# Two hybrid decoder layers: each layer's rstd folded into the rotary tables, q and k copied out of PSUM by ScalarE and rotated on VectorE alone

## The chip, the cores and the metric

The kernel runs on one core of a Trainium2 chip. The time is device time in microseconds (us) of one execution, from start to end. Engines are named as in the profile: PE (TensorE), DVE (VectorE), ACT (ScalarE), POOL (GpSimd), SP (SyncE, which here only issues DMAs). They run side by side, each through its own list of instructions in order, and wait for one another by semaphores. L163 is line 163 of the kernel before.

## The reference

x is 512 positions of 2048 channels in float32, and there are two layers. Cut to what is touched:

```
for l in range(2):
    h = rms_norm(x, pre_norm_g[l])
    proj = h @ w_in[l]                      # 2048 x 6656, cut into the ten groups below
    rq, rk, rv, rg, dq, dk, dv, dg, lx, lg  # retention, diff attention, RG-LRU
    ro  = retention(rope(rq), rope(rk), rv)             # 6 heads of 128, chunks of 128
    do  = diff_attention(rope(dq), rope(dk), dv, lam)   # 4 heads, q and k in two halves of 64
    lru = rg_lru(conv4(lx), gates)                      # 768 channels, scan over positions
    mixed = concat(rms_norm(ro) * silu(rg), rms_norm(do) * g * silu(dg), lru * silu(lg))
    x = x + rms_norm(mixed @ w_out[l], post_norm_g[l])

def rope(x):        # cos, sin: per position and channel pair
    x1, x2 = split(x, 2)
    return concat(x1 * cos - x2 * sin, x2 * cos + x1 * sin)
```

rms_norm multiplies each position by a reciprocal root mean square, called rstd below. The kernel multiplies the unscaled x (times the gain) by w_in and applies rstd to the product.

## The kernel before

**Passes.** A layer is 18 passes over weights: dv, dq, dk, lx0, lx4, lx8, rq0, rq4, rq8 (`A_` and `B_` in the list `seq`, by the name of the group and the first of its tiles of 128 channels), rv0, rv4, rv8, dg, and for w_out o0, o1, o2, o3a, o3b. rq0, rq4 and rq8 hold the 12 tiles of rq and rk. A pass is 8 chunks of 24 matmuls (128 x 512 results) that accumulate into up to four PSUM banks named `big`. In form A (dq, dk, lx, rq) the weights are stationary and a bank is 128 channels by 512 positions; in form B it is 128 positions by 512 channels.

**Weights.** Each fp32 product is done as three fp32r ones, from a high part and a remainder of both operands. `load_chunk` brings a chunk (512 KB) by a DMA on SP, ACT casts it to `whi` (L163), and DVE subtracts to get `wlo` (L164). There are three buffers of each; a chunk is loaded two chunks ahead of its use.

**Order.** A scheduler orders DVE, ACT, POOL and PE; chunk loads and evacuations have high priority. SP's order is written by hand. The first chunks go round the banks, the last two (three, for passes with fewer banks) bank by bank, and as a bank is complete its evacuation is issued. The next pass takes the banks in the same order.

**Side work.** All else (rotary work, attention, LRU, retention heads) is written as generators in one queue, `side`. After every second (chunk, bank) step, so after 12 matmuls, `pump` runs the first generator up to its next `yield`; the second starts when the first is done. So the number of yields of a piece sets when everything behind it in the queue starts. `drain` empties the queue ahead of the output passes. The tables and `layer_rstd` are side work too, at a layer's start, and `ready` sets the flag that `wait_ready` looks at.

**What the change touches.** `evac_rope` takes q or k of a tile out of PSUM (`qk`), with rstd along the positions (`rsb`, 128 x 512, the same in each partition), and queues `rope`. That multiplies by the sine with the halves swapped (`rt`, L399 and L400 for retention with halves of 64, L404 for diff attention with quarters of 32; on DVE), multiplies by the cosine (L401, L405; POOL), and adds (L406; POOL for retention, DVE for diff). For diff attention `stack` then makes the fp32r parts: two casts on ACT, and for k two more half tiles, moved by POOL's `tensor_scalar` (L427, L428), and remainders `kl` on DVE (L432, L433).

**What stands around it.** `diff_attention` forms scores `sc` in PSUM (L462, L463), a masked maximum on DVE (L465), the exponential `pr` on ACT (L471), and transposes `wT` (L485), copied by ACT (L487). `evac_lx` and `evac_lg` take the LRU's banks out by a DVE multiply with `rsb`; lg then has a sigmoid on ACT (L642), whose table differs from the exponential's, so that ACT loads a table (`ACT_TABLE_LOAD`) between them. `lru_half` makes the gates (L567 to L616: casts `gwh`, `xh` and sigmoids on ACT, `xc`, `xl` on DVE, matmuls `gate`). The retention heads begin behind rv0's pass, and `evac_rvg` takes rv out by turns on DVE and ACT (L738).

Of the kernel before, what the change touches and what calls it, by code (L numbers as in the profile page):

```python
# [18 lines left out]
ALU = mybir.AluOpType  # L19
# [21 lines left out]
LEAD, SLEAD, RLEAD = 4, 8, 6  # L41
# [54 lines left out]
def tile_hybrid_trunk(ctx, tc, x, xt, pos, ppar, lamqk, w_in, gw, w_out, postg, cp, cm, out):  # L96
# [285 lines left out]
    def lead(n):  # L382
        for _ in range(n):
            yield

    def ready():
        prepared[0] = True
        yield

    def wait_ready():  # L390
        while not prepared[0]:
            yield


    def rope(st, raw, dst, key, kind):
        yield from wait_ready()
        t2 = U("rt2")
        if kind == "ret":
            V.tensor_tensor(t2[64:128, :], raw[0:64, :], sin_r[0:64, :], op=ALU.mult)  # L399
            V.tensor_tensor(t2[0:64, :], raw[64:128, :], sin_r[64:128, :], op=ALU.mult)  # L400
            G.tensor_tensor(raw, raw, cos_r, op=ALU.mult)  # L401
        else:
            for a, b in ((0, 32), (32, 0), (64, 96), (96, 64)):
                V.tensor_tensor(t2[b:b + 32, :], raw[a:a + 32, :], sin_d[a:a + 32, :], op=ALU.mult)  # L404
            G.tensor_tensor(raw, raw, cos_d, op=ALU.mult)  # L405
        (G if kind == 'ret' else V).tensor_tensor(raw, raw, t2, op=ALU.add)  # L406
        if kind == "ret":
            dst[key] = raw
        yield
        if kind != "ret":  # L410
            yield from stack(st, raw, key, kind)
# [3 lines left out]
    def stack(st, nat, h, kind):  # L415
        lo_, hi_ = slice(0, 64), slice(64, 128)
        s0, s1 = U("st", F32R), U("st", F32R)
        if kind == "dq":
            A.copy(s0[lo_, :], nat[lo_, :])
            A.copy(s1[hi_, :], nat[hi_, :])  # L420
            V.tensor_tensor(s0[hi_, :], nat[lo_, :], s0[lo_, :], op=ALU.subtract)
            V.tensor_tensor(s1[lo_, :], nat[hi_, :], s1[hi_, :], op=ALU.subtract)
            st["dqs"][h] = (s0, s1)
        else:
            A.copy(s0[lo_, :], nat[lo_, :])
            A.copy(s1[hi_, :], nat[hi_, :])
            G.tensor_scalar(s0[hi_, :], nat[lo_, :], 1.0, 0.0, op0=ALU.mult, op1=ALU.add)  # L427
            G.tensor_scalar(s1[lo_, :], nat[hi_, :], 1.0, 0.0, op0=ALU.mult, op1=ALU.add)  # L428
            k0, k1 = U("kl", F32R), U("kl", F32R)
            G.memset(k0[hi_, :].bitcast(F32), 0.0)  # L430
            G.memset(k1[lo_, :].bitcast(F32), 0.0)
            V.tensor_tensor(k0[lo_, :], nat[lo_, :], s0[lo_, :], op=ALU.subtract)  # L432
            V.tensor_tensor(k1[hi_, :], nat[hi_, :], s1[hi_, :], op=ALU.subtract)  # L433
            st["dks"][h] = (s0, s1, k0, k1)
        yield

    def evac_rope(st, ps, dst, key, kind):
        raw = U("qk")
        V.tensor_tensor(raw, ps, st["rsb"], op=ALU.mult)
        side.append(rope(st, raw, dst, key, kind))  # L440


# [372 lines left out]

    def new_state():
        return {k: {} for k in ("h", "dq", "dk", "dqs", "dks", "dv", "dg", "lx", "lg", "lh", "rq", "rk", "rv", "rg", "ro",
                                "mix", "y", "ry", "xr", "pg")}

    states = [new_state() for _ in range(DEPTH)]  # L820
    for l in range(DEPTH - 1):
# [77 lines left out]
    def start_norm():  # L899
        nc.sync.dma_start(cmt, cm)  # L900
        acc = {}
        for k in range(NK):
            j = int(k % NPOOL == 1)
            sq = U("xsq")
            A.activation(sq, xts[k], AF.Square)
            if j in acc:
                (V, G)[j].tensor_tensor(acc[j], acc[j], sq, op=ALU.add)
            else:
                acc[j] = sq
            if k % 2:  # L910
                yield
        ps = SM("ssx")
        for tb in range(NT):
            for j in range(2):
                T.matmul(ps[:, tb:tb + 1], lhsT=acc[j][:, tb * P:(tb + 1) * P], rhs=ones,
                         start=(j == 0), stop=(j == 1))
        V.tensor_copy(ssx[:, :, 0], ps[:, :NT])
        V.memset(ssx[:, :, 1:], 0.0)
        yield from layer_rstd(st)
# [15 lines left out]
    for l in range(DEPTH):  # L935
        st = states[l]
        if l == 0:
            side.append(chain(start_norm(), lead(LEAD), tables(), layer_params(0), layer_params(1), ready()))
        else:
            side.append(chain(lead(RLEAD), layer_rstd(st)))  # L940
        for i, (p, tasks) in enumerate(layer_passes[l]):
            if i == 13:
                drain()
            if i in (13, 14, 15, 16):
                n = i - 13
                st["pg"][n] = U("pg")
                nc.sync.dma_start(st["pg"][n], postg[l, n * S:(n + 1) * S].partition_broadcast(P))
            if i == 15:
                side.append(load_x(l, st))
            run_pass(p)  # L950
            for t in tasks:
                side.append(t())
# [97 lines left out]
```

## Time and profile before

| | |
|---|---|
| median of three runs | 1665.0 us (1664.53 to 1665.46) |
| the profiled execution | 1666.37 us, span 1664.4 us, mean granted clock 0.993 |
| busy, share of the span | PE 98%, PEld 81%, DVE 56%, ACT 38%, POOL 16% |
| weights' DMAs | 287 of 512 KB on SP's queue, 3.5 to 3.6 us from issue to landing |
| mean DMA rate | 107 GB/s |

The span runs from the first to the last instruction; 2.0 us of the execution lie around it. PEld is the weight load of PE, which runs beside its matmuls. A row of instruction groups reads: line, engine, operation, out<-in, shapes, count, then busy us and mean ns of one, then idle time of the engine just before them and what ended it.

By the trace layer 0's passes run from 6 to 840 us and layer 1's from 840 to 1655; the rotary work of diff attention lies around 101 to 200 and 931 to 1005, that of retention around 440 to 480 and in the rq and rv passes of layer 1 (1142 to 1323).

### The profile page before, as it was taken

What the parts mean: (1) busy time and instruction counts of PE and PEld (TensorE: products, weight loads), DVE (VectorE), ACT (ScalarE), POOL (GpSimd) and SP (SyncE); (2) the same over time, 40 slices, a digit from 0 to 9 for tenths busy, and PEclk for the clock granted to TensorE, in tenths of its full rate; (3) what the DMA queues carried; (4) which work ended last, traced back from release to release, by engine and by line L of the source; (5) the groups of instructions that cost most, each with busy time, mean ns of one, the idle gap of its engine ahead of it and who ended that gap; (6) DMA issues with size and microseconds to landing.
All of it is one profiled execution on the core that took longest, in us unless ns stands there. A gap on an engine that the chain in (4) does not pass through costs nothing. (4 is left out here: it accounts for less than half of the span.)

```text
span 1664.4 us, 19440 instructions
## 1 busy us (share of the span) xinstructions
PE 1634.2 (98%) x7541; PEld 1349.5 (81%) x7541; DVE 928.7 (56%) x1474; ACT 626.0 (38%) x966; POOL 259.1 (16%) x216
## 2 busy tenths in 40 slices
PE   9999899999999999999999998999999999999997
PEld 7788788787877888888888887888888888888886
DVE  6767765665674444322772776664677544442336
ACT  6232345457212323222662224346541222332233
POOL 0011400111261110000110131003035301100003
PEclk9999999999999999999999999999999999999999
DMA  7233222232322222344643222222323322223635
GB/s 258 79 92 101 89 64 84 89 96 76 102 76 77 76 89 83 107 146 158 222 159 100 89 89 77 76 84 83 92 86 102 101 73 77 91 96 108 196 124 199
DMA packets 54747, 177.50 MB, mean 107 GB/s; under 512 B 6656, under 2 KB 7680, under 8 KB 54656
## 3 DMA queue, kind: packets, MB, share of 16 engines
q1 hardware_dynamic: 52592, 169.94, 32.2%
q0 software_dynamic: 1920, 6.29, 1.0%
q8 instruction: 59, 0.97, 0.2%
q14 instruction: 32, 0.26, 0.1%
q10 hardware_dynamic: 144, 0.04, 0.0%
HBM read 167.86 MB, written 8.39 MB: 106 GB/s over the span
## 5 line engine op out<-in xcount | busy, mean ns | idle before, releaser
L164 DVE TENSOR_TENSOR wlo<-raw,whi 128x1024 fp32r<-128x1024 f32 (+1 forms) x289 | 370.5, 1286 | 426.7 <-ACT whi L163 412.8
L163 ACT CAST whi<-raw 128x1024 fp32r<-128x1024 f32 (+1 forms) x289 | 302.6, 1049 | 630.2 <-PE big L208 549.1
L208 PE MATMUL big<-hhi,whi 128*128 128x512 f32 x1024 | 402.9, 394 | 1.5 <-DVE lx L635 1.5
L208 PE MATMUL big<-hhi,wlo 128*128 128x512 f32 x1024 | 400.6, 391 | 1.6 <-DVE wlo L164 1.6
L208 PE MATMUL big<-hlo,whi 128*128 128x512 f32 x1024 | 400.0, 391 | 0.0
L208 PE MATMUL big<-whi,hhi 128*128 128x512 f32 x640 | 255.3, 401 | 3.7 <-ACT rv L738 2.6
L208 PE MATMUL big<-wlo,hhi 128*128 128x512 f32 x640 | 252.0, 395 | 2.7 <-DVE wlo L164 2.7
L208 PE MATMUL big<-whi,hlo 128*128 128x512 f32 x640 | 251.6, 393 | 0.0
L208 PEld LDWEIGHTS big<-hhi,wlo 128*128 128x128 f32 x1024 | 192.9, 188 | 42.5 <-DVE wlo L164 2.0
L208 PEld LDWEIGHTS big<-hhi,whi 128*128 128x128 f32 x1024 | 193.0, 188 | 41.7 <-DVE lx L635 2.0
L208 PEld LDWEIGHTS big<-hlo,whi 128*128 128x128 f32 x1024 | 193.0, 189 | 38.8
L208 PE MATMUL big<-wlo,mhi 128*128 128x512 f32 x512 | 199.5, 390 | 0.6 <-DVE wlo L164 0.6
L208 PE MATMUL big<-whi,mlo 128*128 128x512 f32 x512 | 199.8, 390 | 0.0
L208 PE MATMUL big<-whi,mhi 128*128 128x512 f32 x512 | 199.8, 390 | 0.0
L208 PEld LDWEIGHTS big<-wlo,hhi 128*128 128x128 f32 x640 | 121.5, 190 | 29.4 <-DVE wlo L164 3.1
L208 PEld LDWEIGHTS big<-whi,hhi 128*128 128x128 f32 x640 | 121.5, 190 | 28.3 <-ACT rv L738 3.0
L208 PEld LDWEIGHTS big<-whi,hlo 128*128 128x128 f32 x640 | 121.6, 190 | 24.2
L208 PEld LDWEIGHTS big<-wlo,mhi 128*128 128x128 f32 x512 | 96.1, 188 | 21.2 <-DVE wlo L164 1.5
L208 PEld LDWEIGHTS big<-whi,mlo 128*128 128x128 f32 x512 | 96.2, 188 | 19.7
L208 PEld LDWEIGHTS big<-whi,mhi 128*128 128x128 f32 x512 | 96.1, 188 | 19.6
L773 POOL TENSOR_TENSOR ry<-sy,mhalf 128x1 f32<-128x1 f32 x8 | 4.7, 585 | 406.7 <-DVE sy L771 406.7
L471 ACT ACTIVATE pr<-sc,mx 128x128 f32<-128x128 f32 (+3 forms) x64 | 33.3, 525 | 75.7 <-DVE mx L468 75.6
(212 smaller groups left out, 1530.0 us busy)
## 6 DMA issues: line engine op xcount, KB each, us to landing
raw<-in_w_in SPq DMA_DIRECT2D x207, 512.0 KB, 3.6
raw<-in_w_out SPq DMA_DIRECT2D x80, 512.0 KB, 3.5
xT<-in_xt SPq DMA_DIRECT2D x16, 256.0 KB, 6.6
xr<-in_x SPq DMA_DIRECT2D x16, 256.0 KB, 5.5
xs<-y POOLq DMA_DIRECT2D x16, 256.0 KB, 3.5
xr<-xs SPq DMA_DIRECT2D x16, 256.0 KB, 5.5
pg<-in_postg SPq DMA_DIRECT2D x8, 256.0 KB, 3.9
out<-y POOLq DMA_DIRECT2D x8, 256.0 KB, 4.5
```

The lines of the kernel that those rows point to most:

```text
L163: last_copy[0] = A.copy(hi[:, a:b, :], raw[:, a:b, :])
L164: V.tensor_tensor(lo[:, a:b, :], raw[:, a:b, :], hi[:, a:b, :], op=ALU.subtract)
L208: T.matmul(ps[b], lhsT=lhsT, rhs=rhs, start=(cnt[b] == 0), stop=(cnt[b] == total - 1))
L471: A.activation(p[:, :n], sc[c][:, :n], AF.Exp, bias=mx[:, c:c + 1], scale=0.125, accum_out=sums[:, h:h + 1])
L773: G.tensor_tensor(st["ry"][tb], ms, mhalf[:, :1], op=ALU.pow)
```

## The change

Once a layer's rstd is there, `scale_tables` multiplies the four tables by `rsb` into tiles of the layer (DVE, four instructions). q and k then leave PSUM by a plain copy on ACT, and `rope` uses the scaled tables, all on DVE: for each tile the sine parts, the cosine multiply and the addition. The two half tiles of k that POOL moved are copied by ACT. `rope` waits for the layer's tables (`turned`) instead of for `ready`, and the scaled tables are given back after 8 diff and 12 retention tiles. The rope of diff attention has one yield more, in the middle of its four quarters.

```
+    def scale_tables(st):
+        yield from wait_ready()
+        for name, table in (("cos_d", cos_d), ("sin_d", sin_d), ("cos_r", cos_r), ("sin_r", sin_r)):
+            st[name] = U(name)
+            V.tensor_tensor(st[name], table, st["rsb"], op=ALU.mult)
+            if name[0] == "s":
+                yield
+        st["turned"] = 0
     def rope(st, raw, dst, key, kind):
-        yield from wait_ready()
+        while st["turned"] is None:
+            yield
         t2 = U("rt2")
         if kind == "ret":
-            V.tensor_tensor(t2[64:128, :], raw[0:64, :], sin_r[0:64, :], op=ALU.mult)
-            V.tensor_tensor(t2[0:64, :], raw[64:128, :], sin_r[64:128, :], op=ALU.mult)
-            G.tensor_tensor(raw, raw, cos_r, op=ALU.mult)
+            cos, sin = st["cos_r"], st["sin_r"]
+            swaps, w = ((0, 64), (64, 0)), 64
         else:
-            for a, b in ((0, 32), (32, 0), (64, 96), (96, 64)):
-                V.tensor_tensor(t2[b:b + 32, :], raw[a:a + 32, :], sin_d[a:a + 32, :], op=ALU.mult)
-            G.tensor_tensor(raw, raw, cos_d, op=ALU.mult)
-        (G if kind == 'ret' else V).tensor_tensor(raw, raw, t2, op=ALU.add)
+            cos, sin = st["cos_d"], st["sin_d"]
+            swaps, w = ((0, 32), (32, 0), (64, 96), (96, 64)), 32
+        for a, b in swaps:
+            V.tensor_tensor(t2[b:b + w, :], raw[a:a + w, :], sin[a:a + w, :], op=ALU.mult)
+            if w == 32 and a == 32:
+                yield
+        V.tensor_tensor(raw, raw, cos, op=ALU.mult)
+        V.tensor_tensor(raw, raw, t2, op=ALU.add)
+        st["turned"] += 1
...
     def stack(st, nat, h, kind):
...
-            G.tensor_scalar(s0[hi_, :], nat[lo_, :], 1.0, 0.0, op0=ALU.mult, op1=ALU.add)
-            G.tensor_scalar(s1[lo_, :], nat[hi_, :], 1.0, 0.0, op0=ALU.mult, op1=ALU.add)
+            A.copy(s0[hi_, :], nat[lo_, :])
+            A.copy(s1[lo_, :], nat[hi_, :])
...
     def evac_rope(st, ps, dst, key, kind):
         raw = U("qk")
-        V.tensor_tensor(raw, ps, st["rsb"], op=ALU.mult)
+        A.copy(raw, ps)
         side.append(rope(st, raw, dst, key, kind))
...
-            side.append(chain(start_norm(), lead(LEAD), tables(), layer_params(0), layer_params(1), ready()))
+            side.append(chain(start_norm(), lead(LEAD), tables(), layer_params(0), layer_params(1), ready(), scale_tables(st)))
...
-            side.append(chain(lead(RLEAD), layer_rstd(st)))
+            side.append(chain(lead(RLEAD), layer_rstd(st), scale_tables(st)))
```

PE and SP have the same instructions as before, but the extra yields shift side work against the passes: the first scores of layer 0 move from early in lx4's pass to behind its fifth chunk, the gates from rq0's second chunk to its seventh, the first retention heads from rv4's second chunk to its seventh; in layer 1 the first scores move by two chunks, within lx0's pass. The order in which the instructions stand, at three places (line numbers of the changed kernel are higher; `x2` marks two rows alike):

DVE at layer 0's retention ropes, in rv0's pass, between two weight remainders; before:

```order
L164 TENSOR_TENSOR wlo_3671<-raw_3669,whi_3670 128x1024
L399 TENSOR_TENSOR rt_700_3687<-qk_2984,sin_r 64x512
L400 TENSOR_TENSOR rt_700_3687<-qk_2984,sin_r 64x512
L399 TENSOR_TENSOR rt_704_3722<-qk_3291,sin_r 64x512
L400 TENSOR_TENSOR rt_704_3722<-qk_3291,sin_r 64x512
L399 TENSOR_TENSOR rt_708_3757<-qk_3314,sin_r 64x512
L400 TENSOR_TENSOR rt_708_3757<-qk_3314,sin_r 64x512
L399 TENSOR_TENSOR rt_712_3792<-qk_3334,sin_r 64x512
L164 TENSOR_TENSOR wlo_3706<-raw_3704,whi_3705 128x1024
```

and now:

```order
L164 TENSOR_TENSOR wlo_3689<-raw_3687,whi_3688 128x1024
L420 TENSOR_TENSOR qk_2878<-qk_2878,rt_707_3740 128x512
L416 TENSOR_TENSOR rt_711_3775<-qk_2897,sin_r_1106 64x512
L416 TENSOR_TENSOR rt_715_3810<-qk_2916,sin_r_1106 64x512
L419 TENSOR_TENSOR qk_2897<-qk_2897,cos_r_1104 128x512
L416 TENSOR_TENSOR rt_715_3810<-qk_2916,sin_r_1106 64x512
L420 TENSOR_TENSOR qk_2897<-qk_2897,rt_711_3775 128x512
L419 TENSOR_TENSOR qk_2916<-qk_2916,cos_r_1104 128x512
L164 TENSOR_TENSOR wlo_3724<-raw_3722,whi_3723 128x1024
```

Three and a half ropes' sine halves stood there; now it is less than two whole ropes.

ACT at the end of lx8's pass in layer 0, ahead of rq0's; before:

```order
L163 CAST whi_2525<-raw_2524 128x1024
L642 ACT_TABLE_LOAD
L642 ACTIVATE lgs_2550<-lg_2548 128x512
L642 ACTIVATE lgs_2567<-lg_2565 128x512
L567 CAST gwh_2571<-gwr_2570 96x384
L163 CAST whi_2537<-raw_2536 128x1024
```

and now:

```order
L163 CAST whi_2399<-raw_2398 128x1024
L661 ACT_TABLE_LOAD
L661 ACTIVATE lgs_2424<-lg_2422 128x512
L490 ACT_TABLE_LOAD
L490 ACTIVATE pr_2437,s_443_2357<-sc_2428,mx_2427 128x512
L490 ACTIVATE pr_2439,s_444_2358<-sc_2431,mx_2427 128x512
L506 COPY wT_2450<-wT_2445 128x512
L520 ACTIVATE dsq_2457<-acc_2266 128x512
L661 ACT_TABLE_LOAD
L661 ACTIVATE lgs_2485<-lg_2483 128x512
L661 ACTIVATE lgs_2502<-lg_2500 128x512
L163 CAST whi_2411<-raw_2410 128x1024
```

The attention of layer 0 now runs into this boundary, so that its exponentials alternate with the sigmoids of lg, each with a table load.

DVE at the end of layer 1's diff ropes, in lx0's pass; before:

```order
L406 TENSOR_TENSOR qk_7381<-qk_7381,rt_1310_7515 128x512
L432 TENSOR_TENSOR kl_7546<-qk_7381,st_7540 64x512
L433 TENSOR_TENSOR kl_7547<-qk_7381,st_7541 64x512
L164 TENSOR_TENSOR wlo_7566<-raw_7564,whi_7565 128x1024
L465 ISA sc_7585,mx_7584<-sc_7585,cmt 128x128
```

and now:

```order
L451 TENSOR_TENSOR kl_7622<-qk_7397,st_7616 64x512
L452 TENSOR_TENSOR kl_7623<-qk_7397,st_7617 64x512
L164 TENSOR_TENSOR wlo_7563<-raw_7561,whi_7562 128x1024
L164 TENSOR_TENSOR wlo_7600<-raw_7598,whi_7599 128x1024
L164 TENSOR_TENSOR wlo_7642<-raw_7640,whi_7641 128x1024
L654 TENSOR_TENSOR lx_7664<-big_7399,rsb_6746 128x512
L484 ISA sc_7669,mx_7668<-sc_7669,cmt 128x128
```

Three weight remainders and a bank's evacuation stand between the last rope and the first scores, where there was one remainder.

More of the change, by code (lines that the diff above doesn't have):

```diff
@@ L392, in wait_ready @@
             yield
+    def scale_tables(st):
[6 more added lines that the diff above has]
+        st["turned"] = 0
     def rope(st, raw, dst, key, kind):
-        yield from wait_ready()
+        while st["turned"] is None:
+            yield
         t2 = U("rt2")
         if kind == "ret":
-            V.tensor_tensor(t2[64:128, :], raw[0:64, :], sin_r[0:64, :], op=ALU.mult)
-            V.tensor_tensor(t2[0:64, :], raw[64:128, :], sin_r[64:128, :], op=ALU.mult)
-            G.tensor_tensor(raw, raw, cos_r, op=ALU.mult)
-        else:
-            for a, b in ((0, 32), (32, 0), (64, 96), (96, 64)):
-                V.tensor_tensor(t2[b:b + 32, :], raw[a:a + 32, :], sin_d[a:a + 32, :], op=ALU.mult)
-            G.tensor_tensor(raw, raw, cos_d, op=ALU.mult)
-        (G if kind == 'ret' else V).tensor_tensor(raw, raw, t2, op=ALU.add)
+            cos, sin = st["cos_r"], st["sin_r"]
+            swaps, w = ((0, 64), (64, 0)), 64
+        else:
+            cos, sin = st["cos_d"], st["sin_d"]
[7 more added lines that the diff above has]
+        st["turned"] += 1
+        if st["turned"] == 8:
+            del st["cos_d"], st["sin_d"]
+        elif st["turned"] == 20:
+            del st["cos_r"], st["sin_r"]
         if kind == "ret":
@@ L817, in new_state @@
         return {k: {} for k in ("h", "dq", "dk", "dqs", "dks", "dv", "dg", "lx", "lg", "lh", "rq", "rk", "rv", "rg", "ro",
-                                "mix", "y", "ry", "xr", "pg")}
+                                "mix", "y", "ry", "xr", "pg")} | {"turned": None}
     states = [new_state() for _ in range(DEPTH)]
```

## The prediction

> **What bounds the kernel now.** First the page: span, busy row of the engines, granted clock.
>
> ```profile
> span 1664.4 us, 19440 instructions
> ...
> PE 1634.2 (98%) x7541; PEld 1349.5 (81%) x7541; DVE 928.7 (56%) x1474; ACT 626.0 (38%) x966; POOL 259.1 (16%) x216
> ```
>
> PE is busy 98% of the span and no other engine is near it, so the time is PE's work plus PE's holes. The change leaves PE's instructions alone; it can only open or close holes. The view of waits for PE names them:
>
> ```profile
> PE sc L462 <- ACT pr L471: 5.2, 3, 2.8
> PE big L208 <- DVE wlo L164: 4.9, 4, 2.7
> PE big L208 <- ACT rv L738: 2.6, 1, 2.6
> PE big L208 <- DVE lx L635: 1.5, 1, 1.5
> ```
>
> Columns: total us, times, longest. Next I looked for the places, and asked the windows view for each: length, busy time of each engine (instructions), granted clock, DMA share, GB/s.
>
> ```profile
> 176.00:182.00 6.00, 4.40 (x20) 3.32 (x19) 5.13 (x7) 1.13 (x2) 2.29 (x4) 1.00 0.11 16
> 192.00:200.00 8.00, 4.74 (x25) 3.63 (x24) 6.38 (x11) 4.39 (x7) 5.74 (x5) 1.00 0.43 128
> 200.00:212.00 12.00, 11.44 (x60) 9.02 (x59) 7.50 (x32) 4.77 (x19) 0.00 (x0) 1.00 0.28 87
> 430.00:440.00 10.00, 10.00 (x46) 8.29 (x45) 2.31 (x2) 1.45 (x2) 0.00 (x0) 1.00 0.35 105
> 470.00:481.00 11.00, 8.30 (x30) 6.35 (x29) 9.93 (x5) 1.05 (x1) 8.74 (x5) 0.84 0.30 90
> 500.00:510.00 10.00, 7.41 (x26) 5.65 (x25) 5.65 (x6) 3.77 (x6) 3.59 (x3) 0.84 0.34 105
> 1000.00:1012.00 12.00, 8.52 (x29) 6.71 (x28) 6.87 (x21) 6.27 (x14) 2.66 (x4) 0.72 0.37 124
> ```
>
> 430 to 440 is an undisturbed stage: PE busy 10.00 of 10, clock 1.00. A disturbed one loses its length less PE's busy time, and beside it (1 - clock) x length, because after the long waits the granted clock stays low for a while. 470-481: 2.70 + 1.76 = 4.46. 500-510: 2.59 + 1.60 = 4.19. 1000-1012: 3.48 + 3.36 = 6.84. 176-182: 1.60; 192-200: 3.26; 200-212: 0.56, all three at full clock. Together 20.9 us; this is what the change can win here. In 192-200, 470-481 and 176-182 POOL and DVE are busy together, and there the durations of DVE give the cause. Groups of one stretch, before and during POOL's work (430 to 453, then 453 to 476; busy us, mean ns):
>
> ```profile
> L400 DVE TENSOR_TENSOR rt<-qk,sin_r 64x512 f32<-64x512 f32 x2 | 1.4, 686 | 0.0
> ...
> L400 DVE TENSOR_TENSOR rt<-qk,sin_r 64x512 f32<-64x512 f32 x6 | 9.1, 1516 | 0.1
> L164 DVE TENSOR_TENSOR wlo<-raw,whi 128x1024 fp32r<-128x1024 f32 x4 | 8.3, 2096 | 0.1
> L399 DVE TENSOR_TENSOR rt<-qk,sin_r 64x512 f32<-64x512 f32 x6 | 8.0, 1340 | 0.2
> ```
>
> And single ones in order of time (start, duration, engine):
>
> ```profile
> 443.98 0.69 DVE L400 TENSOR_TENSOR rt<-qk,sin_r 64x512 f32<-64x512 f32 x1
> ...
> 444.75 1.30 POOL L401 TENSOR_TENSOR qk<-qk,cos_r 128x512 f32<-128x512 f32 x1 [15.54 <-DVE rt L400]
> ...
> 456.21 1.73 POOL L401 TENSOR_TENSOR qk<-qk,cos_r 128x512 f32<-128x512 f32 x1 [1.39 <-PE big L208]
> ...
> 456.80 1.69 DVE L400 TENSOR_TENSOR rt<-qk,sin_r 64x512 f32<-64x512 f32 x1
> ```
>
> The same instruction takes 0.69 us while POOL stands idle (15.54 up to 444.75) and 1.69 inside POOL's multiply of 456.21; the weight remainder wlo takes 2096 ns in that stretch (1290 on average, below). Eight of a chunk's 24 matmuls read wlo, so a DVE at half speed makes wlo late: the hole at 470-481.
>
> **The change part by part.** Prices, from the groups (busy, mean ns, then idle before):
>
> ```profile
> L164 DVE TENSOR_TENSOR wlo<-raw,whi 128x1024 fp32r<-128x1024 f32 x287 | 369.1, 1290 | 426.7 <-ACT whi L163 412.8 <-DMA xr<-xs 7.6 <-DMA xr<-in_x 3.4
> L439 DVE TENSOR_TENSOR qk<-big,rsb 128x512 f32<-128x512 f32 x40 | 27.4, 688 | 22.7 <-PE big L208 22.5
> L406 DVE TENSOR_TENSOR qk<-qk,rt 128x512 f32<-128x512 f32 x16 | 11.1, 691 | 17.4 <-POOL qk L405 17.4
> L401 POOL TENSOR_TENSOR qk<-qk,cos_r 128x512 f32<-128x512 f32 x24 | 44.0, 1834 | 95.6 <-DVE rt L400 92.8 <-PE big L208 2.8
> L406 POOL TENSOR_TENSOR qk<-qk,rt 128x512 f32<-128x512 f32 x24 | 42.6, 1776 | 1.9
> L405 POOL TENSOR_TENSOR qk<-qk,cos_d 128x512 f32<-128x512 f32 x16 | 23.6, 1473 | 169.7 <-DVE rt L404 167.4 <-issue 2.3
> L428 POOL TENSOR_SCALAR st<-qk 64x512 fp32r<-64x512 f32 x8 | 9.6, 1202 | 0.6
> L427 POOL TENSOR_SCALAR st<-qk 64x512 fp32r<-64x512 f32 x8 | 8.6, 1070 | 6.7 <-DVE qk L406 5.8 <-issue 0.9
> L425 ACT CAST st<-qk 64x512 fp32r<-64x512 f32 x8 | 5.0, 621 | 42.1 <-DVE qk L406 42.1
> L487 ACT COPY wT<-wT 128x512 f32<-128x512 f32 x8 | 4.7, 585 | 3.1 <-PE wT L485 3.1
> L642 ACT ACT_TABLE_LOAD x5 | 6.4, 1283 | 2.7 <-DVE lg L640 2.6
> ```
>
> *POOL* loses 40 cos multiplies, 24 additions and 16 half copies: 44.0 + 42.6 + 23.6 + 9.6 + 8.6 = 128.4 of its 259.1 us. Its own time buys nothing; what counts is that DVE's neighbours return to their undisturbed durations, and that a rope no longer waits for POOL (17.4 us of DVE idle behind L405).
>
> *DVE* loses 40 PSUM multiplies (27.4) and gains 8 table multiplies (two layers, four tables; 8 x 0.69 = 5.5), 40 cos multiplies (27.6) and 24 additions (16.6): +22.3. Against that, in 453-476 alone twelve halves shrink from 17.1 to 12 x 0.686 = 8.2. So DVE's total stays within some 20 us of its 928.7, 56% of the span. In the retention ropes' stage the changed order has at most eight rope instructions between two wlo of the main phase, 8 x 0.69 = 5.5 plus one undisturbed wlo of at most 1.29, against the chunk in which they are needed:
>
> ```profile
> 455.93 1.06 ACT L163 CAST whi<-raw 128x1024 fp32r<-128x1024 f32 x1 [4.38 <-PE big L208]
> ...
> 461.37 1.06 ACT L163 CAST whi<-raw 128x1024 fp32r<-128x1024 f32 x1 [4.38 <-PE big L208]
> ```
>
> one chunk every 5.44 us. That is an excess of 1.3 in a chunk or two, with three weight buffers ahead; before, seven rope halves at some 1.43 (the mean of the two rows) and a wlo of 2.10 made 12.1. I cost the DVE side of this at nothing; if that cover fails, wlo is late again by the excess, 1 to 3 us.
>
> *The rstd factor* goes into the tables once a layer, in the stage of the first passes, where nothing waits for the 4 x 0.69 us but the ropes themselves; nothing.
>
> *ScalarE* gains 40 PSUM copies (nearest row L487: PSUM source, 128x512, 585 ns; 23.4 us), 16 half casts (L425, 10.0) and 8 table loads (the order has 40 instead of 32; 10.3): +43.7 on 626, 40%. The total hides under PE; the places don't all. The copy frees the PSUM bank that the next pass needs, and stands in ACT's order behind whatever ACT waits for. Its range: a gain where before a DVE multiply (688) was queued behind wlo, a loss of a whole ACT queue where a gate or softmax stands ahead.
>
> *The moved work.* A rope of diff attention yields once more, so the attention of layer 0 starts some five chunks (27 us) later, in lx4's pass instead of at its start, and the gates and retention heads follow, to rq0 and rv4; layer 1's attention by two chunks. The drain ahead of the output projections stays where it is, so no work is pushed behind the last matmul: the end of the kernel costs nothing either way. But the stall places change. What the shift takes away is in the windows 192-200 (attention start beside POOL's ropes), 500-510 (rv evacuation behind retention heads on ACT) and 1000-1012 (attention start of layer 1), where the cause of the wait can be read:
>
> ```profile
> 1002.52 1.28 ACT L471 ACT_TABLE_LOAD   x1
> ...
> 1005.05 0.39 PE L462 MATMUL sc<-st,st 128*128 128x128 f32 x1 [2.80 <-ACT pr L471]
> ```
>
> There the score matmul waits 2.80 for an exponential that starts behind a table load. In the changed order DVE finishes all ropes of layer 1, then three wlo in a row, ahead of the first scores, so PE has chunk work between them.
>
> What comes instead I walked through by the changed order with the durations above. An attention start costs PE one late probability tile or two (an exp with its 1.28 table load, less the 12 matmuls between two side steps): 1.1 in layer 0 and 1.3 in layer 1. At the boundaries of the LRU and rq passes a copy (0.585) stands behind gate work of 0.6 to 0.7 or a table load of 1.28 on ACT: 1.3 (lx8 to rq0, layer 0), 0.35 (rq4 to rq8), 1.2 (rq0 to rq4, layer 1). The rv evacuation keeps 0.4. Sum 5.65. Each of these six is unseen in the trace; bounds by the nearest rows are nothing (430-440) and 4.19 (500-510, a bank released late by ACT, with its clock). I take values near the lower end because the clock fell only behind waits of 2.6 us and more, and the walked waits are half of that; the upper end goes into the range.
>
> A table load's price decides part of that. In the trace the next instruction starts 1.30 after it:
>
> ```profile
> 100.53 1.28 ACT L294 ACT_TABLE_LOAD   x1
> 101.83 0.63 ACT L294 ACTIVATE sin_r<-ang 64x512 f32<-64x512 f32 x1
> ```
>
> The Trainium skill, "ScalarE: Activation LUTs", section "What ACT_TABLE_LOAD costs", adds a drain of about 1380 ns to every switch, 2.66 us in all; by it, as an estimate, the eight new loads would be 21.3 us of ACT instead of 10.3, and the three at lx8 to rq0 would hold that boundary's copies 4.1 longer. The 1.30 of the row leaves no room for that drain, and I go by the row.
>
> Sum: gone 20.9, new 5.65, net 15.2, taken as 15. The profiled execution took 1666.4 for a span of 1664.4, and the sum is made against it: 1651.4. It is 1.4 above the median of the three runs (1665.0); against that median, 1650.0.
>
> **The rivals.**
>
> *PSUM held by ScalarE (slower).* ACT works in order; the forty copies wait behind sigmoids, exponentials, casts and table loads at five boundaries (lx8 to rq0, rq0 to rq4 and rq4 to rq8 in layer 0; lx8 to rq0 and rq0 to rq4 in layer 1), which before were DVE's. If each costs what 500-510 cost, 4.19, the result is 1650 - 2.85 (what the forecast has there) + 21 = 1668; at 6.84 (as 1000-1012) 1681. I put it at 1672. It decides from (15 + 2.85) / 5 = 3.6 us a place. For it: ACT's idle time 42.1 behind DVE at L425 shows that its queue does stand and wait. Against it: the last two chunks go bank by bank, so a pass's first bank is done 36 matmuls, 8.2 us, before the next pass starts, and its last one is wanted 18 matmuls, 4.1 us, after (by the 5.44 us a chunk); a copy has to be later than that.
>
> *The waits only move (no change).* The wait at 1005 comes from the chain score, exponential, transpose, not from a rope. If such chains reopen at their new places with a low clock, the 20.9 return: 1662 to 1668.
>
> *A part stays.* One of the three long holes keeps its wait and its clock (4.2 to 6.8 us), or table loads hold ACT longer than their row: 1650 + 4 to 11, 1654 to 1661, say 1657. For it: ACT's load rises at just these places.
>
> *POOL is not the cause.* If the half multiplies are slow of themselves, all four DVE instructions of a retention rope would take 1.4, 5.7 together, and a rope can come with every half chunk, 2.72 us: twelve ropes put DVE some 36 us behind, against two chunks (10.9) of weights ahead. The 9.3 of the three POOL windows would not come back, and about 25 would be added: 1650 + 9 + 25 = 1684. Against it: 0.69 and 1.69 in one and the same line.
>
> *More than forecast.* The new waits hide entirely and smaller old holes close too: 1642 to 1645.
>
> **How the numbers follow.** Forecast (gain 10 to 20, 1645 to 1655) 0.53; a part stays 0.20; more 0.07; the waits only move 0.08, all of it within 0.2% (3.3 us, what a measurement of this kernel can tell from none); ScalarE holds PSUM 0.10; POOL not the cause 0.02. Faster 0.53 + 0.20 + 0.07 = 0.80, same 0.08, slower 0.12. The range 1642 to 1664 takes in the first three cases and the lower part of the fourth, a little over 0.8. The forecast alone: 1645 to 1655.
>
> **What would show it.** Right: POOL near 130 us, the retention halves (64x512 by sin_r) near 0.69 on average, ACT near 670, no clock slice below full between 460 and 520 nor near 1005, and PE's waits for wlo and rv gone from the list, with the score waits below 2 us. Wrong: PE waiting for ACT's qk copies in the big rows, a hole of over 2.5 us at a pass boundary between lx8 and rq8, a table load with more than 1.3 us behind it, or half multiplies still above 1 us with POOL idle.
>
> The clock is what doubles a mistake. It fell after holes of 2.59 and 2.70 us here and stayed at full after those of 1.60. The Trainium skill, "TensorE: Matmul & The Clock Gate", section "Why this matters for your kernels", warns of gaps over about 3 us; by that rule a new wait under 3 us would cost only itself, while by these rows one of 2.6 costs 1.6 to 1.8 more.

## The result and the profile after

The changed kernel takes 1642.87 us (median of four runs, 1641.95 to 1643.69), the kernel before 1665.23 in the same set. The ratio is 0.9863, 95% interval 0.9851 to 0.9874: 22.4 us faster, where 15 were forecast. The time lies in the stated range of 1642 to 1664, at its lower end. The profiled execution took 1641.95, 0.9 below the median.

The page of the changed kernel, span and busy row:

```profile
span 1640.2 us, 19391 instructions
...
PE 1625.5 (99%) x7541; PEld 1343.5 (82%) x7541; DVE 905.0 (55%) x1506; ACT 668.4 (41%) x1030; POOL 130.5 (8%) x136
```

The span is 24.2 us shorter. PE's busy time fell by 8.7 with the same 7541 matmuls: those are the stretches at half clock that are gone, some 1.8 us of them at the start (below). PE's idle time, span less busy, fell from 30.2 to 14.7. POOL is at 130.5 and ACT at 668.4, as worked out (130.7 and about 670). DVE has 32 instructions more and 23.7 us less.

PE's waits after:

```profile
PE ssx L934 <- DVE xsq L926: 1.4, 1, 1.4
...
PE big L208 <- DVE wlo L164: 0.8, 2, 0.5
PE sc L481 <- ACT pr L490: 0.8, 2, 0.7
```

The score waits of 5.2 are 0.8, wlo's 4.9 are 0.8, the rv wait of 2.6 and the lx wait of 1.5 are no longer in the list (the prediction had wlo gone from it too); and no wait for a copy of q or k has come in. The windows view by stage shows where the time went. Before (start to the end of dv; lx passes, rq passes and rv passes of layer 0; lx passes of layer 1):

```profile
0.00:57.40 57.40, 53.51 (x222) 41.98 (x223) 35.48 (x50) 31.58 (x48) 6.12 (x11) 0.94 0.56 196
...
144.40:307.00 162.60, 156.81 (x762) 129.83 (x761) 107.40 (x237) 68.11 (x133) 32.08 (x30) 1.00 0.26 80
307.00:450.60 143.60, 143.02 (x626) 115.42 (x625) 91.47 (x113) 76.04 (x99) 26.75 (x19) 1.00 0.29 90
450.60:611.90 161.30, 156.01 (x764) 131.02 (x763) 88.00 (x124) 41.40 (x57) 44.45 (x28) 0.98 0.26 79
...
974.30:1142.00 167.70, 163.17 (x780) 135.40 (x779) 109.04 (x240) 71.97 (x141) 25.61 (x26) 0.98 0.25 78
```

The same five after:

```profile
0.00:55.40 55.40, 52.44 (x222) 40.37 (x223) 35.10 (x49) 31.17 (x47) 6.12 (x11) 0.97 0.57 203
...
142.50:294.50 152.00, 151.30 (x726) 125.83 (x725) 106.84 (x227) 72.89 (x133) 11.02 (x11) 1.00 0.27 83
294.50:441.00 146.50, 146.50 (x662) 120.14 (x661) 83.20 (x113) 89.72 (x122) 18.07 (x14) 1.00 0.29 91
441.00:593.20 152.20, 152.20 (x764) 128.83 (x763) 90.72 (x154) 44.09 (x62) 8.62 (x8) 1.00 0.26 83
...
955.20:1113.90 158.70, 157.66 (x769) 130.94 (x768) 107.69 (x239) 73.37 (x141) 7.88 (x7) 1.00 0.26 82
```

A stage's length says little, since the moved side work puts 36 matmuls into rq that stood in lx; length less PE busy is what counts. In the last four stages it was 5.79 + 0.58 + 5.29 + 4.53 = 16.2 and is 0.70 + 0 + 0 + 1.04 = 1.7. The two stages at 0.98 lost 6.6 us to the clock (0.02 x 161.3 + 0.02 x 167.7) and are at 1.00. So 21.1 us come from these four stages. The start adds 2.0 (57.4 to 55.4) by a part that the change does not touch: the low clock at 50 us lasted half as long in this execution, 3.4 us instead of 6.8. Every profile of this case shows one of these two lengths there, worth 1.7 or 3.4 us. What sets it is not shown, so a difference of 1.7 us between two profiles below may be no more than this.

DVE in layer 0's retention stage (441 to 497) of the changed kernel, where POOL now stands idle:

```profile
L416 DVE TENSOR_TENSOR rt<-qk,sin_r 64x512 f32<-64x512 f32 x20 | 13.7, 686 | 0.5
L164 DVE TENSOR_TENSOR wlo<-raw,whi 128x1024 fp32r<-128x1024 f32 x11 | 13.4, 1222 | 12.6 <-ACT whi L163 12.5
```

The halves take 686 ns, where the stretch before had 1340 and 1516, and wlo 1222 where it had 2096.

### The profile page after: what moved, and what is told of

Its sections match the earlier page's. It is cut to its first block, busy times and chain, and to the rows that moved or that the text cites. A ratio compares the mean times of both kernels' runs of the same rounds, so it can differ in the third digit from the quotient of the medians.

```text
span 1640.2 us, 19391 instructions
## 1 busy us (share of the span) xinstructions
PE 1625.5 (99%) x7541; PEld 1343.5 (82%) x7541; DVE 905.0 (55%) x1506; ACT 668.4 (41%) x1030; POOL 130.5 (8%) x136
## 5 line engine op out<-in xcount | busy, mean ns | idle before, releaser
L164 DVE TENSOR_TENSOR wlo<-raw,whi 128x1024 fp32r<-128x1024 f32 (+1 forms) x289 | 355.7, 1234 | 466.6 <-ACT whi L163 450.5
L208 PEld LDWEIGHTS big<-whi,hlo 128*128 128x128 f32 x640 | 120.7, 189 | 23.7
L416 DVE TENSOR_TENSOR rt<-qk,sin_d 32x512 f32<-32x512 f32 x64 | 43.7, 683 | 3.6 <-ACT qk L458 2.5
```

Source lines behind the costliest of these rows:

```text
L164: V.tensor_tensor(lo[:, a:b, :], raw[:, a:b, :], hi[:, a:b, :], op=ALU.subtract)
L208: T.matmul(ps[b], lhsT=lhsT, rhs=rhs, start=(cnt[b] == 0), stop=(cnt[b] == total - 1))
L416: V.tensor_tensor(t2[b:b + w, :], raw[a:a + w, :], sin[a:a + w, :], op=ALU.mult)
```

## The experiments

The change has four parts: the rope on DVE alone, the extra yield, the tables with ScalarE's copies, and k's halves on ScalarE. Seven kernels put them in or leave them out, so that each ratio to the kernel before can be set against another.

**The rope on DVE alone.** The kernel before with

```
-            G.tensor_tensor(raw, raw, cos_r, op=ALU.mult)
+            V.tensor_tensor(raw, raw, cos_r, op=ALU.mult)
...
-            G.tensor_tensor(raw, raw, cos_d, op=ALU.mult)
-        (G if kind == 'ret' else V).tensor_tensor(raw, raw, t2, op=ALU.add)
+            V.tensor_tensor(raw, raw, cos_d, op=ALU.mult)
+        V.tensor_tensor(raw, raw, t2, op=ALU.add)
```

> The kernel before with one edit: the rope's cosine multiply and addition go from POOL to DVE for all tiles; PSUM evacuation by DVE with rstd, k's halves on POOL and the yields stay, so the side work keeps its places. Theory C (POOL's tensor_tensors slow DVE, and that made the holes): the holes at 179, 194 and 472 (with the low clock behind it) go, 1.8 + 1.7 + 4.5, perhaps the one at 502 (4.2) too; those at the attention starts (198: 1.9; 1002: about 6.8 with the clock) stay. 1652 to 1658. Theory S (the extra yields' shift of the side work is the gain): no change beyond 2 us, 1663 to 1667. If DVE becomes too full instead: above 1667.

1650.48 us, 0.9914 (0.9900 to 0.9927): 14.3 of the 22.4, a little more than theory C's range. Its windows, from the retention ropes to the first retention heads, and at layer 1's attention start:

```profile
465.00:505.00 40.00, 40.00 (x186) 33.38 (x186) 25.50 (x38) 10.56 (x16) 0.00 (x0) 1.00 0.31 98
985.00:997.00 12.00, 10.07 (x45) 8.21 (x45) 7.74 (x23) 6.28 (x14) 2.67 (x4) 0.86 0.38 128
```

The first row has no hole and full clock, so the hole behind wlo and the one at the rv evacuation both went with POOL's work. The attention start of layer 1 stays, at 1.9 of idle and 1.7 of clock (0.14 x 12) instead of 3.5 and 3.4.

**The extra yield alone.** The kernel before with

```
             for a, b in ((0, 32), (32, 0), (64, 96), (96, 64)):
                 V.tensor_tensor(t2[b:b + 32, :], raw[a:a + 32, :], sin_d[a:a + 32, :], op=ALU.mult)
+                if a == 32:
+                    yield
```

> The kernel before with one edit: the extra yield in the rope of diff attention. All else, POOL's share too, as before; the first scores of layer 0 move from lx4's first chunk to its fifth, the retention heads by four chunks, layer 1's first scores by two. Theory C: the holes at 179 and 472 stay (1.8 + 4.5), those at 198, 502 and 1002 (1.9 + 4.2 + 6.8) may go: 1652 to 1662. Theory S: most of the 22 us comes from here, 1642 to 1650.

1658.44 us, 0.9958 (0.9945 to 0.9970), in theory C's range, but not by the holes that theory C named. Its waits:

```profile
PE big L208 <- ACT rv L740: 6.1, 2, 4.3
PE big L208 <- DVE wlo L164: 3.2, 3, 2.8
PE sc L464 <- ACT pr L473: 2.4, 2, 1.7
```

The score waits fell from 5.2 to 2.4, and the rv wait rose from 2.6 to 6.1. The holes at 179 and 472, which were expected to stay, went; the long wait for wlo is now in layer 1, at its retention ropes, where the kernel before had no hole:

```profile
1280.00:1300.00 20.00, 17.16 (x68) 13.65 (x68) 17.00 (x10) 2.57 (x3) 15.16 (x9) 0.91 0.33 100
```

Moving the side work took holes away, made one larger and opened another, as long as POOL (busy 15.16 of these 20 us) stood beside DVE. That the time still fell into the range is luck.

**All but the yield.** The changed kernel with

```
-            if w == 32 and a == 32:
-                yield
```

> The changed kernel without the extra yield in the rope of diff attention: the first scores stand at lx4's second chunk (layer 0) and lx0's fifth (layer 1, as in the kernel before). Theory C: only the attention starts' holes come back (some 2 in layer 0, 3 to 7 in layer 1 with the clock): 1645 to 1652. Theory S: most of the gain is lost, 1656 to 1665.

1646.72 us, 0.9893 (0.9879 to 0.9906), within theory C's range. Its waits, those at the attention starts:

```profile
PE sc L479 <- ACT pr L488: 2.3, 4, 0.7
PE wT L502 <- ACT whi L163: 1.7, 2, 0.8
```

4.0 us, against 0.8 and none in the changed kernel, and no low clock at either place. That is the yield's share on top of the rest, 5.0 us by the two ratios.

**All but the rope on DVE.** The changed kernel with

```
-        V.tensor_tensor(raw, raw, cos, op=ALU.mult)
-        V.tensor_tensor(raw, raw, t2, op=ALU.add)
+        G.tensor_tensor(raw, raw, cos, op=ALU.mult)
+        (G if kind == 'ret' else V).tensor_tensor(raw, raw, t2, op=ALU.add)
```

> The changed kernel with the rope's cosine multiply and the retention addition back on POOL; scaled tables, ScalarE's copies and the yields stay. Theory C: DVE's half multiplies are slow again (mean 1.1 to 1.3 us for the retention halves), wlo is late in the retention ropes' stage, 4 to 10 us of the gain are lost: 1647 to 1653. Theory S: within 2 us of the changed kernel, 1641 to 1645.

1654.2 us, 0.9937 (0.9923 to 0.9950): 12.3 us worse than the changed kernel, more than theory C gave. Not wlo was late this time but rv:

```profile
PE big L208 <- ACT rv L757: 6.2, 2, 4.3
```

The window around it, and then the timeline, DVE's rows before POOL's:

```profile
485.00:502.00 17.00, 10.85 (x35) 8.04 (x34) 16.69 (x15) 4.38 (x7) 14.48 (x9) 0.80 0.18 62
```

```profile
481.88 4.68 DVE L416 TENSOR_TENSOR rt<-qk,sin_r 64x512 f32<-64x512 f32 x3
486.60 0.35 DVE L759 TENSOR_SCALAR rv<-big,rstd 128x128 f32<-128x128 f32 x1
...
482.58 1.74 POOL L419 TENSOR_TENSOR qk<-qk,cos_r 128x512 f32<-128x512 f32 x1
484.40 1.61 POOL L420 TENSOR_TENSOR qk<-qk,rt 128x512 f32<-128x512 f32 x1
```

Three rope halves of DVE take 4.68 us, 1.56 each, with POOL at work all the while, and the 0.35 us evacuation stands behind them. ACT shares the evacuation of a bank with DVE, so the list names ACT's rv as what PE waited for; ACT's own rv of 486.98 had waited 4.73 us for DVE's. 6.2 us of idle and 3.4 of clock (0.20 x 17) in one place.

**POOL's work without its results.** Is DVE slow because POOL works, or did it wait for POOL's results? The changed kernel with work on POOL that nobody waits for:

```
+        if kind == "ret":
+            idle, half = warm.bitcast(F32), S // 2
+            for n in range(4):
+                src = (cos_r if n else t2)[:, :half]
+                if st is states[0]:
+                    G.tensor_tensor(idle, src, sin_r[:, :half], op=ALU.mult)
+                elif st["turned"] < 14:
+                    G.tensor_scalar(idle, src, 1.0, 0.0, op0=ALU.mult, op1=ALU.add)
+                elif n == 0:
+                    G.tensor_scalar(idle, src, 1.0, 0.0, op0=ALU.mult, op1=ALU.add)
+                else:
+                    G.memset(idle, 0.0)
```

> The changed kernel, to which POOL work is added that nobody waits for: after the sine parts of each retention rope POOL does four 128x256 operations into a tile that is read no more. Layer 0: tensor_tensor (two inputs). Layer 1, first half of the tiles: tensor_scalar (one input), second half: one tensor_scalar and three memsets (no input). Theory C (DVE is slowed by POOL's working, not by waiting for its results): the retention halves of layer 0 take 1.1 to 1.6 us on average again, wlo is late, and 4 to 12 us are lost, 1647 to 1655. If instead the waits for POOL's results were the cause: 1641 to 1645, halves at 0.69. In layer 1 the durations of DVE beside tensor_scalar and memset tell whether one input or none slows it too; little time hangs on it there.

1651.5 us, 0.9926 (0.9913 to 0.9940): 10.5 us lost again by the ratios, with no result of POOL in use, and from 440 to 510 DVE has no wait for POOL. DVE's groups in that stage (440 to 500), and the longest of PE's waits behind the start:

```profile
L164 DVE TENSOR_TENSOR wlo<-raw,whi 128x1024 fp32r<-128x1024 f32 x11 | 16.7, 1529 | 5.4 <-ACT whi L163 5.3
L416 DVE TENSOR_TENSOR rt<-qk,sin_r 64x512 f32<-64x512 f32 x17 | 15.1, 891 | 0.4
L431 DVE TENSOR_TENSOR qk<-qk,cos_r 128x512 f32<-128x512 f32 x8 | 8.2, 1024 | 0.1
```

```profile
PE big L208 <- ACT rv L769: 2.1, 1, 2.1
```

The mean of the halves, 891 ns, is below the 1.1 to 1.6 expected (some ran while POOL stood idle); wlo at 1529 and the cosine multiply at 1024 are slow too. The profiled execution is 7.2 us longer than the changed kernel's; 5.4 of that stand between 480 and 520 (3.6 of PE idle, 1.8 of clock), the stage with the added work, and 1.7 are the low clock at the start. The cause holds: DVE is slowed by POOL's working.

**k's halves back on POOL.** The changed kernel with the two `G.tensor_scalar` lines of `stack` in place of the copies on ScalarE.

> The changed kernel with k's two half copies back on POOL as tensor_scalar. If POOL's work slows DVE wherever they meet: the k remainders (kl) take 0.9 to 1.0 us instead of 0.69, and 1 to 4 us are lost, 1644 to 1647. If these sixteen are too few to matter: 1641 to 1644.

1644.41 us, 0.9878 (0.9865 to 0.9892). 2.5 us worse by the ratios, but the interval overlaps that of the changed kernel, so it is not shown apart. The remainders were slowed, one of the two more than the other (885 and 734 ns instead of 689 and 682). But PE did not pay for it: from 60 to 1600 us it is idle for 2.1 us in this profile and in the changed kernel's alike, and the 2.5 us by which the two differ stand ahead of that, 1.8 in the low clock at the start and 0.8 in more idle time there. So the second case of the expectation holds by the trace: these sixteen are too few to matter.

**Without the tables.** The changed kernel with rstd applied by DVE as q and k leave PSUM, as in the kernel before, and so without ScalarE's copies; the other three parts stay.

> The changed kernel without its tables: rstd is applied by DVE as q and k leave PSUM, as before, and ScalarE does not copy them; the rope on DVE alone, k's halves on ScalarE and the extra yield stay. If tables and copies relieve DVE at the pass boundaries (the two runs with them and without the extra yield differ by 3.8 us, of which k's halves may hold a part): 1645 to 1648. If they only move an evacuation from one engine with slack to another: 1641 to 1644. If ScalarE's copies cost (the slower rival of the prediction): below 1641. The clock at 50 us was low for 6.8 us in all three profiles without tables and 3.4 us in all three with them: if the tables set that, 6.8 here, if it is chance, either.

1644.44 us, 0.9880 (0.9867 to 0.9894), 2.8 us from the changed kernel by the ratios, again with overlapping intervals, and between the expected ranges. From 60 to 1600 us PE is idle for 3.7 us instead of 2.1, and the difference is one score wait of 1.7 at 250 us. With the tables go the two yields of `scale_tables`, one chunk of layer 0's side work, so the shift alone may have made that wait; that ScalarE's copies relieve DVE is not shown. The rest is at the start, where the low clock lasted 6.8 us, as it did in the profile of the run before, which has the tables: so the tables do not set it.

**The tables and copies alone.** The kernel before with `scale_tables`, the scaled tables and `A.copy(raw, ps)`; rope on POOL and DVE as before, no yield, k's halves on POOL.

> The kernel before with the tables and ScalarE's copies alone: the rope's cosine multiply and addition and k's halves stay on POOL, no extra yield. The scaling of the tables moves layer 0's side work by one chunk. By the other runs (tables with k's halves were worth some 4 us on top of the rope's move and of the yield): 1660 to 1664. If tables and copies are worth nothing by themselves: 1663 to 1667. If they are the main part after all: below 1656.

1661.97 us, 0.9982 (0.9973 to 0.9991): 3.0 us, as expected from the sum.

The four parts together, in us: by the ratios to the kernel before (of 1665), and by the traces from 60 to 1600 us, that is without the start (PE's idle time, and (1 - clock) x length by windows of 20 us; 23.8 in the kernel before, 2.1 in the changed one). "Alone" is what a part is worth by itself, "last" what it is worth as the last one added.

| part | alone, ratio | last, ratio | alone, trace | last, trace |
|---|---|---|---|---|
| rope on DVE | 14.3 | 12.3 | 15.4 | 10.3 |
| extra yield | 7.0 | 5.0 | 7.0 | 4.0 |
| tables and ScalarE's copies | 3.0 | 2.8 (intervals overlap) | 2.9 | 1.7 |
| k's halves on ScalarE | not run | 2.5 (intervals overlap) | not run | 0.1 |

That the ratios of the last parts sum to 22.6, the whole gain, is partly luck, since they hold the start. In the traces the three parts alone sum to 25.3 and the four last ones to 16.1, of 21.7 in all: rope and yield close some of the same holes. The order of the parts is the same by all four columns.

**ScalarE's slack.** The rival that ended slower rested on ScalarE holding the banks. The changed kernel with

```
-        A.copy(raw, ps)
+        for _ in range(4):
+            A.copy(raw, ps)
```

> The changed kernel with each of the forty copies of q and k out of PSUM done four times by ScalarE (three more of 0.585 us, 70 us of ACT in all). If ScalarE holding banks were near to a wait (the slower rival of the prediction, and the 2.85 us that the forecast gave to three boundaries): PE waits for qk in rows of big at the boundaries of the dq, dk and rq passes, 5 to 20 us, 1648 to 1663. If the banks have the slack of 4.1 to 8.2 us that the bank-by-bank ends of the passes give: within 1.5 us of the changed kernel, 1641.5 to 1644.5, and no wait for qk in the list.

1650.6 us, 0.9912 (0.9899 to 0.9926): 8.2 us lost by 70 us of added ACT work. It falls into the first of the two ranges, so at some places the slack is smaller than 4 to 8 us. The wait, and its longest place, at the start of dk in layer 0:

```profile
PE big L208 <- ACT qk L459: 2.8, 3, 1.6
```

```profile
106.39 0.50 PE L208 MATMUL big<-hhi,whi 128*128 128x512 f32 x1 [1.59 <-ACT qk L459]
```

There the copies stand on ACT between the sines of the tables, behind a table load. The changed kernel's own trace has the one copy of the third and of the fourth bank of dq here:

```profile
96.36 0.59 ACT L458 COPY qk<-big 128x512 f32<-128x512 f32 x1 [2.13 <-PE big L208]
...
101.16 0.59 ACT L458 COPY qk<-big 128x512 f32<-128x512 f32 x1
```

The banks are done 2.72 us apart, so the fourth at about 99.1, but ACT comes to it 2.1 us later. PE takes it 18 matmuls into dk, at about 103.0 or later, and the copy is done at 101.75. So it has 1.2 us or more to spare, well below the 4.1 that PE's order alone gives. The other two waits for qk stand in layer 1, at the start of dk (0.5) and of lx0, behind dk (0.75). At the boundaries to and within the rq passes, where the forecast had put 2.85 us, even four copies bring no wait for qk; there the longer queue on ACT costs one gate wait of 0.9. These waits are some 4 of the 8.2 us. In the profile 1.4 more stand at the end of layer 0 (PE's hT waiting for DVE's hlo) and 1.3 at the start, neither shown to hang on the copies; the rest was not placed. The slower rival of the prediction needed 3.6 us at each of five places.

**Later still.** The changed kernel with `lead(LEAD + 3)` in layer 0 instead of `lead(LEAD)`.

> The changed kernel with three side steps more at the start of layer 0 (8.2 us): its first scores stand at lx4's end instead of behind the fifth chunk, its retention heads begin with rv8 instead of at rv4's end. If later is better of itself: 1638 to 1642. If the gain of the extra yield hangs on the chunk in which the attention and the retention heads begin: 1644 to 1652, with a hole of 1 to 3 us at the boundary lx4 to lx8 or at rv8.

1646.07 us, 0.9889 (0.9874 to 0.9904). The time lies in the second range, but the hole that was to make it did not come: no new wait over 0.7 us is in the profile's list of PE's waits, and none went that was worth it. The median is 4.3 us by the ratios above the changed kernel's, with intervals that touch. In the profile the low clock at the start (6.8 us instead of 3.4) is 1.7 of that, and PE's idle time from 60 to 1600 us 0.7 (2.8 instead of 2.1); the rest is not explained. Later is not better of itself; that the gain hangs on the chunk is not shown by this run either.

**Two attempts on the first hole.** PE waits 1.4 us for the sums of squares at 47 us in every profile so far. The changed kernel with a `yield` ahead of those matmuls (and one step less behind them):

> The changed kernel with the sum of squares' matmuls in layer 0 one side step (12 matmuls, 2.7 us) later, and one side step less between them and the tables. The hole of 1.6 us at 47 us should go, since the squares are done 1.4 us after PE asks for them. If the low clock behind it (3.4 us at half, 1.7 us) comes from the hole: 1639 to 1640.5. If it comes from the small matmuls themselves: 1640.5 to 1642. If later rows of dv then wait for rstd: above 1643.

0.9877 (0.9862 to 0.9892), no gain. The scheduler left the eight matmuls where they were, and the wait is the same 1.4, so this run says nothing on its question. Then the changed kernel with all the sums on DVE (and so four matmuls over them instead of eight):

```
-            j = int(k % NPOOL == 1)
+            j = 0
...
```

> The changed kernel with all sums of squares of the start on DVE: POOL's three 128x512 additions go to it, and the matmuls over them are four instead of eight. If DVE is slowed there by POOL as in the ropes (seven additions took 7.3 us instead of 4.8), nine undisturbed ones take 6.2 and the hole at 47 us shrinks from 1.6 to about 0.5: 1640.5 to 1642.5. If POOL's share was a relief: the hole grows to 2.5 to 3 and the time to 1643.5 to 1647.

0.9874 (0.9860 to 0.9887), no gain either. The wait for the squares is gone, and one for the broadcast of rstd came:

```profile
PE rsb L375 <- DVE rb L374: 2.1, 1, 2.1
```

```profile
40.77 7.85 DVE L926 TENSOR_TENSOR xsq<-xsq,xsq 128x512 f32<-128x512 f32 x10
```

Ten additions take 7.85 us, 0.79 each, where in the changed kernel seven took 7.28, partly beside POOL: the lesson held for DVE, but PE asked for the next link of the same chain. No version beat the changed kernel.

## Why the prediction was right, and where it was off

*What bounds it.* PE's holes, and the clock behind them, carried the time, and what changed came from there: 21.1 of the span's 24.2 us in the four stages, 2.0 at the start. Right.

*The holes that go.* The six windows named, 20.9 us, all closed. The stages' own sums are 16.2 idle and 6.6 clock, 22.8, so 1.9 more went that were not counted: the smaller waits at the gates and in the attention of layer 1.

*The cause.* POOL's work halving DVE's speed was read from two rows of one instruction, 0.69 and 1.69. The rope on DVE alone and the unused POOL work show it, with 14.3 gained and 10.5 lost. That the hole at 500 to 510 had this cause as well was not seen: the prediction filed it under the moved work, by the name in the list (ACT's rv), though its own row has POOL busy for 3.59 us there. The retention ropes of layer 0 did not end at 480, as the part on the time before has it; POOL worked on some from 493 to 503.7. DVE's rows, then POOL's and ACT's, in the kernel before:

```profile
502.72 2.03 DVE L164 TENSOR_TENSOR wlo<-raw,whi 128x1024 fp32r<-128x1024 f32 x1
504.67 0.34 DVE L740 TENSOR_SCALAR rv<-big,rstd 128x128 f32<-128x128 f32 x1
...
501.53 2.13 POOL L406 TENSOR_TENSOR qk<-qk,rt 128x512 f32<-128x512 f32 x1
...
505.05 0.37 ACT L738 ACTIVATE rv<-big,rstd 128x128 f32<-128x128 f32 x1 [1.84 <-DVE rv L740]
```

ACT's rv waited 1.84 us for DVE's, which stood behind a wlo slowed to 2.03 by POOL. The yield alone made this hole larger (2.6 to 6.1), the rope on DVE alone removed it. The list named the engine that came last; DVE's queue behind it was the reason.

*What comes instead.* This is the term that was mis-sized: 5.65 us, measured 1.7 in the four stages, old leftovers included. The attention starts were near (0.7 and 1.0, the idle time of the two lx stages, against 1.1 and 1.3). The boundary terms, 1.3 + 0.35 + 1.2 + 0.4, are zero in the stages' rows of layer 0, and layer 1's rq passes have 0.1. There the walk had put copies behind ACT's gate work and made that a wait, without taking off the slack that the staggered ends of a pass give, which the prediction itself holds against its slower rival. That slack is not always the 4.1 to 8.2 us given there (at the start of dk 1.2 or more are left), but by the four-copies run the rq places bear three more copies, 1.76 us, without a wait for qk. With 3.9 less here and 1.9 more that went, 15.2 becomes 21.0, which is the stages' sum (21.1) told by the prediction's terms; the measured gain is 21.0 to 24.8 by its interval, and some 2 of it may be the start.

*Table loads.* Eight more, as said, and on the path they cost little. At the boundary where the exponentials alternate with lg's sigmoids:

```profile
287.02 1.28 ACT L661 ACT_TABLE_LOAD   x1
288.31 0.63 ACT L661 ACTIVATE lgs<-lg 128x512 f32<-128x512 f32 x1
```

The next instruction starts 1.29 after the load. The drain of 1380 ns that the Trainium skill adds ("ScalarE: Activation LUTs", "What ACT_TABLE_LOAD costs") is not there in this trace either.

*The clock.* The prediction said that it falls only behind holes of 2.6 us and more. That is wrong: in the run with the rope on DVE alone it fell behind two holes of about 1.1 and 0.8 within two microseconds (985 to 997, granted 0.86), and at the start it is low in every profile, behind a hole of 1.4 (2.1 where the squares stood on DVE alone). The last was there to see in the trace of the kernel before (45 to 57: 1.44 idle, granted 0.72). It did no harm to the sum here, since no new long holes came. The Trainium skill ("TensorE: Matmul & The Clock Gate", "Why this matters for your kernels") warns of gaps over about 3 us; by these rows that is not a safe bound.

*The rivals.* ScalarE holding PSUM, POOL not being the cause, and the waits moving on: none came. The yield alone was nearest to the last, with a hole that grew where it put the retention heads' start, as long as POOL still worked there. The case "more than forecast" (1642 to 1645, given 0.07) is where the time lies, 2 us below the forecast's own 1645 to 1655: the range held because it took in that case.

## What to carry to other kernels

A second elementwise engine is not free capacity: before work is put on POOL, compare the duration of one DVE instruction while POOL is idle and while it works, and count the slowdown of all that DVE does in that stretch with two inputs in SBUF. When a wait names an engine that does little, look at whose queue its own instruction was waiting on. And a wait found by walking an order is only one if the lateness exceeds the slack that the staggered ends of the stage give; work that slack out first, then price.

## What the runs showed of the hardware

The slowdown of DVE goes by the POOL instruction beside it. In the run with unused POOL work, where all of POOL's added operations are 128x256, DVE's rows before POOL's (two inputs, then one, then a memset):

```profile
456.05 1.11 DVE L416 TENSOR_TENSOR rt<-qk,sin_r 64x512 f32<-64x512 f32 x1
...
1229.19 0.77 DVE L416 TENSOR_TENSOR rt<-qk,sin_r 64x512 f32<-64x512 f32 x1
...
1230.69 0.88 DVE L431 TENSOR_TENSOR qk<-qk,cos_r 128x512 f32<-128x512 f32 x1
...
1275.06 0.69 DVE L416 TENSOR_TENSOR rt<-qk,sin_r 64x512 f32<-64x512 f32 x1
...
455.55 3.36 POOL L424 TENSOR_TENSOR warm<-cos_r,sin_r 128x256 f32<-128x256 f32 x3
...
1228.70 2.33 POOL L426 TENSOR_SCALAR warm<-cos_r 128x256 f32<-128x256 f32 x3
...
1274.55 1.05 POOL L430 MEMSET warm<- 128x256 f32 x3
```

An instruction of 0.69 us takes 1.11 beside a POOL operation with two inputs, 0.77 to 0.88 beside one with one, and 0.69 beside a memset. Beside the 128x512 operations of the kernel before it took up to 1.69, so the size of POOL's operation counts as well as its kind. The Trainium skill, "GPSIMD Engine Reference", section "1. Specifications", has POOL share its SBUF interfaces with DVE, in contention with DVE instructions of two SBUF inputs; the halves, the cosine multiply and wlo are such, and the runs agree. A DVE multiply that takes one of its two inputs from PSUM ran beside POOL's multiply of 444.75 (1.30 us long, in the prediction) and kept its 0.69:

```profile
445.28 0.69 DVE L439 TENSOR_TENSOR qk<-big,rsb 128x512 f32<-128x512 f32 x1 [0.61 <-PE big L208]
```

How the two engines share is seen where they work back to back, in the kernel before, DVE's rows before POOL's:

```profile
458.52 1.67 DVE L399 TENSOR_TENSOR rt<-qk,sin_r 64x512 f32<-64x512 f32 x1
460.20 1.69 DVE L400 TENSOR_TENSOR rt<-qk,sin_r 64x512 f32<-64x512 f32 x1
...
458.02 1.62 POOL L406 TENSOR_TENSOR qk<-qk,rt 128x512 f32<-128x512 f32 x1
459.60 1.74 POOL L401 TENSOR_TENSOR qk<-qk,cos_r 128x512 f32<-128x512 f32 x1
```

POOL's end at 459.64 and 461.34, DVE's at 460.19 and 461.89. Each half ends 0.55 us behind one of POOL's, which is less than its own 0.69, and POOL is slowed too (1.62 and 1.74 against 1.30). That looks like taking turns, instruction by instruction, rather than both running at a lower speed throughout. POOL's spans are rough and no run was made to test it, so it stays a reading of these rows.
